# A hybrid decoder layer on one core: q's transposes, the planner's POOL prices and slab releases, and the sums of the last norm

## The chip, the core and the metric

The kernel runs on one core of a Trainium2 (trn2) chip. The metric is the device time of one execution in microseconds (us); runs are compared by their median. The engines are TensorE (PE: matmuls, and PEld for its weight loads), VectorE (DVE), ScalarE (ACT), GpSimd (POOL) and SyncE (SP), which here only issues DMAs.

## The reference

One layer for 1024 tokens of width 1024, in float32:

```python
h   = rmsnorm(x, norm_mix_w)
p   = h @ w_in                       # q, k, v, z (4 heads x 128), a, b, lru_x, lru_gate
q, k, v = silu(causal_conv4(qkv));  q = l2norm(q);  k = l2norm(k)
o   = gated_delta_rule_chunked(q, k, v, g, beta)
o   = rmsnorm(o, gdn_norm_w) * silu(z)
lru = rg_lru(causal_conv4(lru_x)) * gelu(lru_gate)
x   = x + concat(o, lru) @ w_out
u   = relu(rmsnorm(x, norm_mlp_w) @ w_ff1)
x   = x + (u * u) @ w_ff2
out = rmsnorm(x, final_norm_w)
```

The chunked delta rule needs, per head, the inverse of a unit lower triangular matrix built from k, and then a scan over chunks whose state is a 128x128 matrix. The l2 norm of q is not applied to q: its sum of squares per token goes into the norm of the output o.

## The kernel before, in words

All data lie transposed, with channels on the partitions and tokens along the row, in two halves of 512 tokens (hf 0 and 1). Float32 precision in the big products comes from splitting each operand into a high and a low part, three matmuls of 128x512 for each 128x128 block of weights (tiles w, xh and xl; results pj in the first projection, po in the second, pf and p in the MLP).

The stages are the input norm, the first projection (with the four heads and the recurrent channels woven in), the second projection, and the MLP, which forms its products from sums and differences of blocks in fewer multiplications.

Nothing is issued while the layer is written down. Every call is recorded in a `Plan` as an operation with its reads and writes, and `Plan.emit` (L285) then sets the order: it keeps a clock of its own for each engine, gives each operation a price (`price`, L264), adds a lag between engines, and at each step issues the operation that can start first, by its due time among those that start about equally early. So the order on each engine is fixed before the kernel runs, and an instruction that the planner thought ready can hold up everything behind it on that engine if its input is late. All instructions carry the line of the one call that issues them (L376); rows are told apart by their tiles. Three things of the planner matter here:

- `admit` (L296) adds `SLACK` to the ready time of a PE operation with a due time from 30 to 1000 (the small ones of the heads) that depends on another engine.
- A POOL step is priced by its row length n: `return 0.2 + 0.0021 * n` (L283).
- The on-chip buffers are 84 slabs of 128x512 float32 (tag "s") and 8 PSUM banks (tag "m"). When the last user of a tile has been placed, its slab goes back at the planner's end of that user plus 0.2 (L382). A tile that takes the slab next then waits, in the kernel, for that last user.

One head goes through these functions: `gd_k` (k transposed by PE into psK, squares and a scaled copy kd on ACT), `gd_u` (psA = k k^T on PE, U on DVE), `invert32` and `rows32` (the 32x32 diagonal blocks go by way of DRAM into the slabs N0 and N1; POOL works through them in 31 rounds of a product into tm and a difference on V, of which the first 16 read N0 and the rest N1; the result goes by way of DRAM into Y), `gd_inv` (32x32 blocks of Y transposed on DVE into YT, then small matmuls psP, psZ and psT double the block size), `gd_q` (psB = k q^T, at on DVE, and q transposed into psQ by four PE transposes per half so that ACT can sum squares per token into pn), `gd_v` (v transposed by `turn`) and `gd_scan` (matmuls pvs and psO, eight chunks one after another). The tile n1B is the scale of the input norm: DVE multiplies each finished pj by it into p, which frees pj's PSUM bank; y is then the convolution on DVE.

`turn` (L671) transposes 128x512 without PE: a DVE transpose of 32x32 blocks, four DMAs to DRAM that put the blocks in their places, and one DMA back. Before the change it is used for v and for o.

At the end, the last two blocks of 256 tokens of the MLP's output are finished in PE groups of p; for each, DVE adds p into u (tile u), ACT squares (sq), and `normed` sums five tiles of squares over the channels with matmuls by ones (n3p: the four new ones and ss, the squares of the other half of the channels), two 128x1 outputs for each tile and each matmul two instructions; then come a square root and its correction (n3r, ms, rst), its broadcast by PE (n3b), eight DVE products into ot and the DMAs of outT.

Of the kernel before, what the change touches and what calls it, by code (L numbers as in the profile page):

```python
# [13 lines left out]
P = 128  # L14
# [18 lines left out]
LOOK = 4  # L33
AHEAD = 100
TAIL = 4
SLACK = 1.3
LAND = 2.0
LATE = 2.5
SMALL = ("bv", "tr")
# [29 lines left out]
def lag(a, b):  # L69
    return LAG[a, b] if (a, b) in LAG else LAG_FROM[a] + (0.12 if b == "pe" else 0.0)  # L70
# [114 lines left out]
class Plan:  # L185
# [77 lines left out]
    @staticmethod  # L263
    def price(e, method, args, kw):  # L264
        out = kw.get("out", args[0] if args else None)
        src = [v for k, v in kw.items() if isinstance(v, View) and k in ("in_", "in0", "in1", "data0")]
        shape = out.shape if isinstance(out, View) else src[0].shape
        n = 1
        for d in shape[1:]:
            n *= d  # L270
        if e == "sy":
            return n * shape[0] * 4 / 300e3
        psum = any(v.root.tag == "m" for v in src)
        ptr = sum(isinstance(kw.get(k), View) for k in ("scalar", "scalar1", "scale", "bias"))
        if e == "ve":
            if method == "reciprocal":
                return 0.06 + 0.0066 * n
            return 0.067 + n * (0.00104 if method in TWO or psum else 0.00052) + 0.06 * ptr
        if e == "ac":
            return 0.0008333 * n + (0.051 if psum else 0.094) + 0.093 * ptr + (0.093 if "accum_out" in kw else 0.0)  # L280
        if method == "memset":
            return 0.036 + 0.00083 * n
        return 0.2 + 0.0021 * n  # L283

    def emit(self, engines, caps):  # L285
        ops = self.ops
# [6 lines left out]
        slots = {t: [(0.0, k) for k in range(n)] for t, n in caps.items()}  # L293
        table, dma = None, 0.0

        def admit(o):  # L296
            for e in o.engines:
                late = SLACK if e == "pe" and o.due < 1000.0 and o.due > 30.0 else 0.0
                ready[e].append((max([d.end + lag(d.eng, e) + (late if d.eng != "pe" else 0.0) for d in o.deps], default=0.0), o))

        def loads(o):

            return o.table is not None and o.table != table and not (o.table == "any" and table in WITH_TANH)
# [44 lines left out]
        for _ in range(len(ops)):  # L348
            pick = choose(True) or choose(False)
            if pick is None:  # L350
                left = [o for o in ops if o.eng is None and not o.wait]
                raise RuntimeError("no room: " + ", ".join(f"{o.engines}.{o.calls[0][0]}:{[r.nm for r in o.roots if r.real is None]}" for o in left[:30])
                                   + str({t: len(s) for t, s in slots.items()}))
            e, s, o = pick
            for x in o.engines:
                ready[x] = [q for q in ready[x] if q[1] is not o]
            for r in o.roots:
                if r.real is None:
                    sl = slots[r.tag]
                    r.slot = max((x for x in sl if x[0] <= s), default=min(sl))  # L360
                    sl.remove(r.slot)
                    r.real = r.make(r.slot[1])
            c = o.cost[e]
            if e == "sy":
                small = any(r.tag in SMALL for r in o.roots)
                free[e] = s + (0.62 if small else 0.45)
                dma = max(dma, free[e] + 0.65) + c
                o.end = dma + (LATE if small else LAND)
            else:
                if loads(o):  # L370
                    table = "exp" if o.table == "any" else o.table
                    c += LOAD
                free[e] = o.end = s + c
            o.eng = e
            for method, args, kw in o.calls:
                getattr(engines[e], method)(*[v.ap() if isinstance(v, View) else v for v in args],  # L376
                                            **{k: v.ap() if isinstance(v, View) else v for k, v in kw.items()})
            for r in o.roots:
                r.users -= 1
                r.end = max(r.end, o.end)  # L380
                if not r.users:
                    slots[r.tag].append((r.end + 0.2, r.slot[1]))  # L382
            for q in o.next:
                q.wait -= 1
                if not q.wait:
                    admit(q)
# [4 lines left out]
def layer(ctx: ExitStack, tc: tile.TileContext, xT, win, wba, prm, cst, wga, wgx, wout, w1, w2, out):  # L391
# [3 lines left out]
    pl = Plan()  # L395
    pe, ve, ac, gp, sy = (pl.engine(n) for n in engines)
# [9 lines left out]
    def slab(nm, dt=F32):  # L406
        return pl.tile(sp, [P, 512], dt, "s", nm)
# [4 lines left out]
    def bank(nm):  # L412
        return pl.tile(mpool, [P, 512], F32, "m", nm)

    def small(nm, shape, bufs=2, dt=F32):
        caps[nm] = bufs
        n = 4
        for d in shape[1:]:
            n *= d
        return pl.tile(cp if n % LINE else bp, shape, dt, nm, nm)  # L420
# [44 lines left out]
    def con(nm):  # L465
        o, w = CST[nm]
        return cs[:, o:o + w]

    ident = con("ident")
# [71 lines left out]
    def when(i):  # L541

        return 14.0 * i
# [127 lines left out]
    def turn(x, nm):  # L671

        y = slab(nm + "t")
        ve.transpose(out=y.rearrange("p (a x) -> p a x", x=32), in_=x.rearrange("p (a x) -> p a x", x=32))
        d = pl.tile(dpool, [P, 512], F32, "tr", nm + "d", True)
        dv = d.rearrange("(j r) (c i x) -> r c j i x", r=32, c=4, i=4)
        for i in range(4):
            sy.dma_start(out=dv[:, :, :, i, :], in_=y[32 * i:32 * i + 32].rearrange("p (c j x) -> p c j x", c=4, j=4))
        z = slab(nm)
        sy.dma_start(out=z, in_=d)  # L680
        return z
# [62 lines left out]
    def gd_q(h, hf):  # L744
        S = HD[h]
        EG, DT = S["qg"][hf], S["DT"][hf]
        kT, qT = store[4 + h, hf], store[h, hf]
        psB = bank("psB")
        with pl.unit(0.86):
            for c in range(4):  # L750
                ks = slice(c * P, (c + 1) * P)
                pe.matmul(psB[:, ks], lhsT=kT[:, ks], rhs=qT[:, ks], start=True, stop=True)
        at = S["at"][hf] = slab("at")
        ve.tensor_tensor(out=at, in0=psB, in1=DT, op=ALU.mult)
        S["last"] = S.get("last", []) + [pl.ops[-1]]
        ve.tensor_tensor(out=EG, in0=EG, in1=qT, op=ALU.mult)
        psQ = bank("psQ")
        with pl.unit(0.44):
            for c in range(4):
                pe.transpose(psQ[:, c * P:(c + 1) * P], qT[:, c * P:(c + 1) * P], ident)  # L760
        pn = S["pn"]
        for c in range(4):
            n = hf * 4 + c
            ac.activation(out=small("osq", [P, P], 2), in_=psQ[:, c * P:(c + 1) * P], func=AF.Square, accum_out=pn[:, n:n + 1])
        if hf == 1:
            ve.tensor_scalar(out=pn, in0=pn, scalar1=EPS, scalar2=EPS * P, op0=ALU.add, op1=ALU.mult)
# [236 lines left out]
    with pl.at(due=-2000.0):  # L1003
        for hf in range(2):
            hs = slice(hf * 512, hf * 512 + 512)
            ps0 = [bank(f"g0_{i}") for i in range(2)]
            ss = slab("ss1")
            for k in range(KT):
                pl.due = -2000.0 + 10 * k + 100 * hf
                if hf == 0:  # L1010
                    xraw[0, k] = slab("xraw")
                    sy.dma_start(out=xraw[0, k], in_=xT[k * P:(k + 1) * P, hs])
                    if k in (0, 2, 4):
                        n = 4 if k == 4 else 2
# [101 lines left out]
    ss = pair("ss2")  # L1116
# [31 lines left out]
    for n, d in enumerate(DO):  # L1148
        i = len(MT) + n
        t = when(i)  # L1150
        split(i + 1)
        for hf in range(2):
# [6 lines left out]
            with chain(t + 7 + 7 * hf):  # L1159
# [3 lines left out]
                x = bm[d, hf] = slab("bm")  # L1163
# [55 lines left out]
    for g in range(NG):  # L1219
        t = tf(g)  # L1220
        ps, y = {}, {}
# [121 lines left out]
    def plus(x, y):  # L1343
        ve.tensor_tensor(out=x, in0=y, in1=x, op=ALU.add)
# [40 lines left out]
    def squares(x, n=512):  # L1385
        y = slab("sq3")[:, 0:n]
        ac.activation(out=y, in_=x, func=AF.Square)
        return y
# [6 lines left out]
    for st, prods in enumerate(STAGES):  # L1395
        tail = TAIL if st == 3 else 0
        pd = {}
        for g0 in range(0, NG, 2):
# [6 lines left out]
            for d in range(4):  # L1405
                for i in prods:
# [10 lines left out]
                    with chain(ts(st, g0) - 100):  # L1417
                        if i in (1, 7, 5):
                            x = {1: p1, 7: u3, 5: p5}[i][d] = slab(f"p{i}_")
# [10 lines left out]
            for x, k, g in residual[st]:  # L1430
                if g in gs:
                    with chain(ts(st, g) + 3):
                        plus(x[k[0] % 4], load_x2(*k, st, g))
                        if x is p5:
                            y = squares(p5[k[0] % 4])
                            if k[0] == 4:
                                ss = y
                            else:
                                plus(ss, y)
        t = begin[st] + 87  # L1440
# [7 lines left out]
        if st == 2:  # L1448
            with chain(t - 40):
                s1 = None  # L1450
                for x in [p1[d] for d in range(4)] + [u3[d] for d in range(4)]:
                    y = squares(x)
# [6 lines left out]
    t = ts(3, NG - TAIL)  # L1459
# [5 lines left out]
    for o in (0, 256):  # L1465
        qs = slice(o, o + 256)
        parts = []
        for d in range(4):
            ps = bank("p2")[:, 0:256]
            for g in range(NG - TAIL, NG):  # L1470
                with pl.at(due=10000.0 + t + o / 50 + 0.1 * d), pl.unit(PIECE / 2):
                    mm3(ps, wsl(g, 3, d), tuple(x[:, qs] for x in UU[g, 3]), g == NG - TAIL, g == NG - 1)
            with chain(t - 100):
                x = u2[d][:, qs]
                plus(x, ps)
                parts.append((squares(x, 256), t))
        parts.insert(1, (ss[:, qs], t))
        X = [u2[d][:, qs] for d in range(4)] + [p5[d][:, qs] for d in range(4)]
        normed(X, parts, 512 + o, 256, t + o / 50, [4, 5, 6, 7, 0, 1, 2, 3], True)

# [64 lines left out]
```

## Time and profile before

| | us |
|---|---|
| median of 3 runs | 1110.3 |
| runs | 1108.43, 1110.3, 1110.89 |
| the profiled execution | 1107.9 |
| its span in the trace | 1105.8 |
| PE busy | 1087.3 |
| DVE busy | 864.8 |
| ACT busy | 552.1 |
| POOL busy | 100.5 |

The mean granted clock of PE over the span is 0.993 of full speed. "Busy" counts time in which an engine works on an instruction; it says nothing of the clock, so a PE at half clock is busy too. The rest of the profile is in the rows below.

### The profile page before, as it was taken

What the parts mean: (1) busy time and instruction counts of PE and PEld (TensorE: products, weight loads), DVE (VectorE), ACT (ScalarE), POOL (GpSimd) and SP (SyncE); (2) the same over time, 40 slices, a digit from 0 to 9 for tenths busy, and PEclk for the clock granted to TensorE, in tenths of its full rate; (3) what the DMA queues carried; (4) which work ended last, traced back from release to release, by engine and by line L of the source; (5) the groups of instructions that cost most, each with busy time, mean ns of one, the idle gap of its engine ahead of it and who ended that gap; (6) DMA issues with size and microseconds to landing.
All of it is one profiled execution on the core that took longest, in us unless ns stands there. A gap on an engine that the chain in (4) does not pass through costs nothing. (4 is left out here: it accounts for less than half of the span.)

```text
span 1105.8 us, 15998 instructions
## 1 busy us (share of the span) xinstructions
PE 1087.3 (98%) x5399; PEld 895.7 (81%) x5399; DVE 864.8 (78%) x1672; ACT 552.1 (50%) x1134; POOL 100.5 (9%) x282
## 2 busy tenths in 40 slices
PE   9999989999999999999999999999999999999996
PEld 7788867888787878888888888888888888888886
DVE  7878665797779776598988888887965767865796
ACT  8559634545485955453333333333444544564442
POOL 0004857026000000000000000000000000000000
PEclk9999989999999999999999999999999999999998
DMA  7133513233212144424544444434856565677382
GB/s 239 39 96 86 125 27 103 68 89 97 78 58 58 39 152 133 153 95 147 197 146 158 146 160 143 171 140 174 283 179 220 180 206 184 206 237 241 125 296 84
DMA packets 124225, 159.17 MB, mean 144 GB/s; under 512 B 56392, under 2 KB 59120, under 8 KB 124144
## 3 DMA queue, kind: packets, MB, share of 16 engines
q1 hardware_dynamic: 124144, 158.16, 44.3%
q8 instruction: 42, 0.69, 0.3%
q14 instruction: 39, 0.32, 0.1%
HBM read 115.11 MB, written 43.01 MB: 143 GB/s over the span
## 5 line engine op out<-in xcount | busy, mean ns | idle before, releaser
L376 PE MATMUL pj<-xh,w 128*128 128x512 f32 x704 | 244.9, 406 | 0.5 <-DVE p L376 0.5
L376 PEld LDWEIGHTS pj<-xh,w 128*128 128x128 f32 x704 | 133.1, 189 | 28.6 <-DVE p L376 1.1
L376 PE MATMUL pj<-xl,w 128*128 128x512 f32 x352 | 138.2, 393 | 0.0
L376 ACT ACTIVATE c<-c 128x512 f32<-128x512 f32 x64 | 40.4, 632 | 85.6 <-DVE c L376 80.7
L376 PE MATMUL po<-mxh,w 128*128 128x512 f32 x256 | 79.3, 390 | 0.8 <-ACT mxh L376 0.8
L376 ACT CAST w<-r 128x512 fp32r<-128x512 f32 (+1 forms) x62 | 51.3, 828 | 54.7 <-PE pf L376 37.8
L376 DVE SCALAR_TENSOR_TENSOR y<-p,pr,y 128x512 f32<-128x512 f32 (+3 forms) x96 | 71.5, 750 | 6.5 <-ACT y L376 4.1
L376 PEld LDWEIGHTS pj<-xl,w 128*128 128x128 f32 x352 | 66.9, 190 | 10.5
L376 DVE TENSOR_TENSOR w<-r,w 128x512 fp32r<-128x512 f32 (+1 forms) x62 | 58.7, 947 | 19.2 <-ACT w L376 18.8
L376 POOL TENSOR_TENSOR tm<-V,N 128x60 f32<-128x60 f32 (+24 forms) x124 | 48.4, 390 | 128.6 <-DMA N<-bn 69.3
L376 PEld LDWEIGHTS po<-mxh,w 128*128 128x128 f32 x256 | 48.0, 188 | 11.1 <-ACT mxh L376 1.2
L376 PE MATMUL po<-mxl,w 128*128 128x512 f32 x128 | 49.9, 390 | 0.7 <-DVE mxl L376 0.7
L376 POOL TENSOR_TENSOR V<-V,tm 128x60 f32<-128x60 f32 (+24 forms) x124 | 45.3, 365 | 9.7
L376 DVE SCALAR_TENSOR_TENSOR c<-c,n2B 128x512 f32<-128x512 f32 x64 | 43.8, 689 | 1.2
L376 PE MATMUL pf<-B5h,w 128*128 128x512 f32 x128 | 42.7, 394 | 0.0
L376 PE MATMUL pf<-B6h,w 128*128 128x512 f32 x128 | 42.3, 390 | 0.0
L376 ACT ACT_TABLE_LOAD x27 | 34.6, 1283 | 3.5 <-DVE y L376 2.4
L376 DVE TENSOR_TENSOR c<-pf,u 128x512 f32<-128x512 f32 x48 | 32.8, 686 | 0.5
L376 ACT CAST v6h<-s 128x512 fp32r<-128x512 f32 x16 | 10.0, 622 | 41.0 <-DVE s L376 41.0
L376 PEld LDWEIGHTS pf<-B5h,w 128*128 128x128 f32 x128 | 24.0, 188 | 6.9 <-DVE c L376 2.0
L376 PE MATMUL p<-u3h,v3h 128*128 128x512 f32 (+1 forms) x80 | 28.4, 355 | 0.7 <-DVE u L376 0.7
L376 PEld LDWEIGHTS po<-mxl,w 128*128 128x128 f32 x128 | 24.0, 188 | 6.0 <-DVE mxl L376 1.0
(512 smaller groups left out, 2976.2 us busy)
## 6 DMA issues: line engine op xcount, KB each, us to landing
w2r<-w SPq DMA_DIRECT2D x112, 256.0 KB, 3.5
ur<-ud SPq DMA_DIRECT2D x112, 256.0 KB, 4.9
r<-w SPq DMA_DIRECT2D x32, 512.0 KB, 3.7
ud<-c SPq DMA_DIRECT2D x64, 256.0 KB, 2.1
ud<-ut SPq DMA_DIRECT2D x48, 256.0 KB, 2.1
r<-win SPq DMA_DIRECT2D x22, 512.0 KB, 4.0
xraw<-xT SPq DMA_DIRECT2D x16, 256.0 KB, 5.2
r<-wout SPq DMA_DIRECT2D x8, 512.0 KB, 4.5
```

Source lines behind the costliest of these rows:

```text
L376: getattr(engines[e], method)(*[v.ap() if isinstance(v, View) else v for v in args], **{k: v.ap() if isinstance(v, View) else v for k, v i ...
```

## The change

It has four parts. `SLACK` becomes 1.0. A POOL step is priced at 0.22 + 0.0023 n. A slab whose last user is on POOL or SP is given back 2.0 after that user's planned end, where it was 0.2. In `gd_q` the four PE transposes into psQ are replaced by `turn`, with the tiles qct (DVE), qcd (DRAM) and qc (back on chip), so that ACT reads squares from a slab. And in the last norm, per block of 256 tokens, the first new square tile takes ss, and then the second and third squares, by three DVE additions; two tiles instead of five go through n3p.

```diff
-SLACK = 1.3
+SLACK = 1.0
...
-        return 0.2 + 0.0021 * n
+        return 0.22 + 0.0023 * n
...
-                    slots[r.tag].append((r.end + 0.2, r.slot[1]))
+                    slots[r.tag].append((r.end + (2.0 if e in ("gp", "sy") else 0.2), r.slot[1]))
...
-        psQ = bank("psQ")
-        with pl.unit(0.44):
-            for c in range(4):
-                pe.transpose(psQ[:, c * P:(c + 1) * P], qT[:, c * P:(c + 1) * P], ident)
+        psQ = turn(qT, "qc")
...
-                parts.append((squares(x, 256), t))
-        parts.insert(1, (ss[:, qs], t))
+                y = squares(x, 256)
+                if d == 0:
+                    plus(y, ss[:, qs])
+                    parts.append((y, t))
+                elif d < 3:
+                    plus(parts[0][0], y)
+                else:
+                    parts.append((y, t))
```

Since prices, waits and buffers feed the planner, the order changes on every engine. Three places follow. In these rows a name in brackets after "waits" is the engine whose count the instruction waits for, and DMAHW with a number is a queue of DMAs.

DVE in the first projection, where the second half of head 0's Y is transposed into YT while POOL works on head 1. Before:

```order
L376 STREAM_TRANSPOSE YT<-Y_0_824 128x256 [waits DMAHW2_49,DMAHW0_49]
L376 SCALAR_TENSOR_TENSOR y_1614<-p,pr,y_1614 128x512 [waits DVE_49] x2
L376 STREAM_TRANSPOSE YT<-Y_1_835 128x256 [waits DMAHW4_49,DMAHW6_49,DMAHW1_49,Pool_49]
L376 TENSOR_TENSOR p<-pj_1586,n1B 128x512 [waits DVE_49,PE_49]
L376 COPY YP<-psP 32x128 [waits PE_49]
```

The same place after; rst, rk, sk and cj are the small factors of head 2, and qct is the new transpose of its q:

```order
L376 STREAM_TRANSPOSE qct<-y_1650 128x512
L376 TENSOR_TENSOR rst<-rk 128x8 [waits DVE_49]
L376 COPY YP<-psP 32x128 [waits PE_49]
L376 SCALAR_TENSOR_TENSOR rst<-rst,sk 128x8 [waits DVE_49]
L376 COPY YP<-psP 32x128
L376 SCALAR_TENSOR_TENSOR rk<-rst,rk 128x8 [waits DVE_49]
L376 STREAM_TRANSPOSE YT<-Y_1_853 128x256 [waits DMAHW6_49,DMAHW0_49]
L376 TENSOR_TENSOR rst<-rk 128x8 [waits DVE_49]
L376 TENSOR_TENSOR p<-pj_1630,n1B 128x512 [waits PE_49]
L376 SCALAR_TENSOR_TENSOR rst<-rst,sk 128x8 [waits DVE_49]
L376 TENSOR_TENSOR at<-psB,DT 128x512 [waits DMAHW7_49,PE_49,Pool_49]
```

The transpose of Y no longer waits for POOL: its slab is another one. The slab that POOL reads as N0 of head 1 now goes to the tile at of head 2, four rows further on, so the wait for POOL stands there, behind the p that frees a PSUM bank.

PE where small matmuls of several heads stand together between two runs of the projection (pj). Before:

```order
L376 MATMUL psK<-cs,y_2523 128x128 [waits DVE_49,PE_49,Activation_49]
...
L376 MATMUL psA<-y_2523 128x128 x4
L376 MATMUL pvs<-vs,Y_0_1484 128x128
L376 MATMUL psT<-cs,Y_0_1901 64x64 [waits DMAHW1_49,DVE_49]
...
L376 MATMUL pvs<-vh,kd 128x128 [waits DVE_49]
L376 MATMUL psO<-vh,at 128x128
L376 MATMUL psP<-YT,U_1_1834 32x32 [waits DVE_49]
...
L376 MATMUL pj_2677<-xh_247,w 128x512 [waits Activation_49]
```

The place in the order after that has the most such waits with no pj between:

```order
L376 MATMUL psK<-cs,y_2277 128x128 [waits DVE_49,Activation_49]
...
L376 MATMUL pvs<-S,y_528 128x128 [waits DVE_49]
L376 MATMUL psO<-S,qg 128x128
L376 MATMUL psA<-y_2277 128x128 [waits DVE_49]
...
L376 MATMUL pvs<-vs,Y_1_853 128x128 [waits DVE_49]
L376 MATMUL psZ<-Y_1_1531,YT 64x64 [waits DMAHW7_49,Activation_49]
...
L376 MATMUL pvs<-vs,Y_0_1516 128x128 [waits DVE_49]
L376 MATMUL pvs<-vh,kd 128x128 [waits DVE_49]
L376 MATMUL psO<-vh,at 128x128
L376 MATMUL pj_2450<-xh_107,w 128x512 [waits DVE_49]
```

From psK to the row ahead of pj seven instructions wait for DVE, ACT or a DMA, where four did before. A line of three dots stands for the further rows of the same matmul.

PE at the end. Before, the last group of p is cut by n3p:

```order
L376 MATMUL n3p<-onesd,sq_11114 128x1 [waits Activation_49]
...
L376 MATMUL p_11106<-u3h,v3h 128x256
L376 MATMUL p_11106<-u3l,v3h 128x256
L376 MATMUL p_11106<-u3h,v3l 128x256
L376 MATMUL n3p<-onesd,sq_11136 128x1 [waits Activation_49]
...
L376 MATMUL n3b<-cs,n3r 128x128 [waits DVE_49,Activation_49]
```

And after:

```order
L376 MATMUL p_11102<-u3h,v3h 128x256
L376 MATMUL p_11102<-u3l,v3h 128x256
L376 MATMUL p_11102<-u3h,v3l 128x256
L376 MATMUL n3p<-onesd,sq_11096 128x1 [waits DVE_49,Activation_49]
...
L376 MATMUL n3b<-cs,n3r 128x128 [waits DVE_49]
...
L376 MATMUL n3p<-onesd,sq_11144 128x1 [waits Activation_49]
...
L376 MATMUL n3b<-cs,n3r 128x128 [waits DVE_49,Activation_49]
```

Both blocks' n3b now stand behind the last p; before, the first block's stood ahead of it, and its eight products into ot ran beside the last p.

## Rows read from the trace of the kernel before

**Rows 1.** The page's part 1: span, then busy us (share) and instructions per engine.

```profile
span 1105.8 us, 15998 instructions
PE 1087.3 (98%) x5399; PEld 895.7 (81%) x5399; DVE 864.8 (78%) x1672; ACT 552.1 (50%) x1134; POOL 100.5 (9%) x282
```

**Rows 2.** Waits of PE: who waited for whom, us in total, times, longest.

```profile
PE psA L376 <- DVE p L376: 3.8, 1, 3.8
...
PE n3b L376 <- DVE n3r L376: 1.4, 1, 1.4
...
PE psP L376 <- DVE S L376: 0.7, 1, 0.7
```

**Rows 3.** Windows: length, busy us of each engine, PEclk, DMA share, GB/s.

```profile
125.00:150.00 25.00, 21.23 (x133) 16.89 (x132) 13.54 (x27) 10.75 (x39) 20.60 (x63) 0.81 0.27 68
200.00:225.00 25.00, 24.25 (x194) 20.38 (x193) 18.23 (x53) 13.04 (x52) 0.00 (x0) 1.00 0.27 66
500.00:700.00 200.00, 200.00 (x883) 164.38 (x882) 173.18 (x281) 76.47 (x129) 0.00 (x0) 1.00 0.46 161
```

**Rows 4.** Finer windows around 140 to 151 us, same columns.

```profile
140.00:141.00 1.00, 0.00 (x0) 0.00 (x0) 0.00 (x0) 0.00 (x0) 0.84 (x3) 0.87 0.00 0
...
147.00:150.00 3.00, 3.00 (x23) 2.33 (x22) 2.35 (x10) 0.66 (x2) 2.45 (x8) 0.50 0.02 5
150.00:151.00 1.00, 1.00 (x18) 0.48 (x16) 0.00 (x0) 0.01 (x1) 0.77 (x4) 0.51 0.00 0
```

**Rows 5.** Timeline of PE: start us, us, instruction, [idle before <-releaser].

```profile
138.58 0.60 PE L376 MATMUL psK<-cs,y 128*128 128x128 f32 x4
142.94 1.44 PE L376 MATMUL psA<-y 128*128 128x128 f32 x5 [3.77 <-DVE p L376]
```

**Rows 6.** Timeline of DVE at the same place.

```profile
135.76 1.61 DVE L376 SCALAR_TENSOR_TENSOR y<-p,pr,y 128x512 f32<-128x512 f32 x2
141.87 0.45 DVE L376 STREAM_TRANSPOSE YT<-Y 128x256 f32<-128x256 f32 x1 [4.49 <-POOL tm L376]
142.24 0.65 DVE L376 TENSOR_TENSOR p<-pj,n1B 128x512 f32<-128x512 f32 x1
```

**Rows 7.** Timeline of POOL at the same place.

```profile
141.53 0.30 POOL L376 TENSOR_TENSOR tm<-V,N 128x64 f32<-128x64 f32 x1
```

**Rows 8.** Instructions on psQ: duration ns min/median/max, first and last start us.

```profile
L376 PE MATMUL psQ<-cs,y x32: 272/273/329, 79.4 to 244.5; 128*128 128x128 f32 x32
```

**Rows 9.** Timeline of PE at a transpose of the same form.

```profile
130.50 0.60 PE L376 MATMUL psK<-cs,y 128*128 128x128 f32 x4
130.94 1.06 PE L376 MATMUL psA<-y 128*128 128x128 f32 x8
```

**Rows 10.** Instructions of v's `turn`, columns as in rows 8.

```profile
L376 SPq DMA_DIRECT2D vsd<-vst x32: 569/627/799, 58.4 to 261.3; - x32
L376 DVE STREAM_TRANSPOSE vst<-y x8: 697/705/711, 57.7 to 258.0; 128x512 f32<-128x512 f32 x8
...
L376 SPq DMA_DIRECT2D vs<-vsd x8: 326/430/557, 64.0 to 265.5; - x8
```

**Rows 11.** The reader of pn at the end of a half's scan.

```profile
L376 DVE SCALAR_TENSOR_TENSOR ro<-so,pn x8: 152/160/164, 194.5 to 366.9; 128x4 f32<-128x4 f32 x8
```

**Rows 12.** The chain that ended last: start us, us, what.

```profile
1088.26 2.13 PE n3p L376 x20
...
1092.82 0.44 PE n3b L376 x4
...
1098.63 0.17 DVE n3r L376
```

**Rows 13.** Timeline of DVE at the end.

```profile
1095.98 0.42 DVE L376 TENSOR_TENSOR u<-p,u 128x256 f32<-128x256 f32 x1
...
1099.65 0.42 DVE L376 TENSOR_TENSOR ot<-n3b,p__9670 128x256 f32<-128x256 f32 x1 [0.86 <-PE n3b L376]
1099.99 0.41 DVE L376 TENSOR_TENSOR ot<-n3b,p__9702 128x256 f32<-128x256 f32 x1
...
1100.99 1.65 DVE L376 SCALAR_TENSOR_TENSOR ot<-u,pr,n3b 128x256 f32<-128x256 f32 x4
```

**Rows 14.** Timeline of PE among small matmuls.

```profile
218.92 0.49 PE L376 MATMUL pvs<-vh,kd 128*128 128x128 f32 x2
...
220.29 0.44 PE L376 MATMUL psP<-YT,U 32*32 32x32 f32 x16 [0.66 <-DVE S L376]
```

## The prediction, written before the changed kernel ran

> **What bounds the kernel now.** I read the page's first part, the waits of PE, the clock by windows, and then the timelines of the three engines at the one long wait. PE is busy 1087.3 of a span of 1105.8 us [rows 1], and in the MLP it is busy 200.00 of 200 us at a granted clock of 1.00 [rows 3]. So time comes from four sources only: work taken off PE, idle time of PE, PE's clock, and the end, where PE has finished. DMAs, loads and stores that move about in the MLP cost nothing as long as PE stays at 200 of 200 there, and I put that reordering at 0.
>
> The idle time is nearly one event. Of the waits of PE the longest by far is psA for DVE's p, 3.8 us [rows 2]. At that place PE ends psK at 139.2 and starts psA at 142.94 [rows 5]. It wants the PSUM bank that p frees; p stands on DVE behind the second transpose into YT, and that waited 4.49 us for POOL's tm [rows 6]. The POOL step at 141.53 is the last round that reads N0 of head 1 [rows 7], and YT sits in the slab that was N0: DVE waited for a buffer, not for data. During the idle time the clock fell: the windows give 0.87 for 140 to 141 us, 0.50 for 147 to 150, and 0.51 for 150 to 151 [rows 4]. So PE worked from 142.94 to about 150.98 at 1.2 GHz, the lower of its two levels, 8.04 us whose work takes half as long at 2.4. The event costs 3.77 + 4.02 = 7.8 us.
>
> **The change part by part.**
>
> *q's transposes.* 32 transposes leave PE [rows 8]. Their 273 ns overlap; four of the same form take 130.94 - 130.50 = 0.44 us from the first to the next work [rows 9]. Eight sets give 8 x 0.44 = 3.5 us off a PE that is otherwise busy in that stage. What comes in: 8 DVE transposes of 0.705 us, 5.6 us in all, and on SP 32 x 0.63 + 8 x 0.43 = 23.6 us of issuing [rows 10]. DVE is busy 13.5 to 18.2 of 25 us in this stage [rows 3], so the 5.6 us, spread over some 170 us, lie in its idle time; the bound is 5.6 if every one stood on PE's path. The squares are read late: the first of q's transposes ran at 79.4, the first reader of pn runs at 194.5 [rows 8, 11], so a landing some us later is covered. ACT's squares read a slab in place of PSUM; ACT is busy 10.8 to 13.0 of 25 us there [rows 3], so a change in their length is hidden. SP has room, about 24 us more over 170, but its queue runs in order and loads of weights and the bn, N and Y copies stand behind q's. I take 0 for the queue; its upper bound is inside the rival on starved PE below.
>
> *Prices and slab releases.* By the order, YT no longer waits for POOL, and p comes ahead of the tile at that now does. I take the whole event away: -3.8 for the idle time and -4.0 for the clock. What is late next at this place is at: it takes the slab that POOL reads until 141.8 in the trace of before; the longer release puts it further behind that, but by how much in time the order doesn't say.
>
> *The smaller `SLACK`.* Small PE work is placed 0.3 us closer behind DVE and ACT, so it may find its input late. The trace of before shows what such a wait costs when it comes: 0.66 us at psP [rows 14]. Nearest row below: that wait goes, -0.7; above: one such wait more for each head, 4 x 0.7 = 2.8. I take one, +0.7, because rows 2 hold just one of that kind in four heads.
>
> *The last norm.* n3p falls from 40 to 16 instructions; 20 took 2.13 us, 0.107 each [rows 12], so 24 are 2.6 us of PE. Not all of it reaches the end, since DVE takes over. Before the last p there were 36 n3p and four n3b instructions (0.44 us), now 8 and none: the last p comes 28 x 0.107 + 0.44 = 3.4 us earlier, and with it the last u, from 1095.98 to about 1092.6 [rows 13]. The three additions per block, about 0.34 to 0.42 each by the spacing and length of DVE's 128x256 products [rows 13], run while PE does p. But behind the last u now stand both blocks' products. From u (0.4) over one small step (0.2) to n3r 1093.2; from n3r to the first ot the old tail took 1099.65 - 1098.63 = 1.0 [rows 12, 13], so 1094.2. Then eight products, 4 x 0.34 + 4 x 0.41 = 3.0, with six small steps of the other block between them at 0.2, 1.2 in all: 1098.4. The other n3b is ready by then (n3r stands three products earlier, 1.2 against 1.0), and the last eight take 3.0: 1101.4 to 1101.5, where it was 1100.99 + 1.65 = 1102.64. Gain 1.1. Bounds: 0, if DVE's steps wait for ACT's squares in turn, and 2.6, the work itself.
>
> *The sum,* on the profiled execution of 1107.9 us (span 1105.8 and 2.1 around it): -3.5 - 3.8 - 4.0 + 0.7 - 1.1 = -11.7, so 1096.2. That execution was 2.4 us below the median of the runs shown, 1110.3; against the median the forecast is 1110.3 - 11.7 = 1098.6.
>
> **The rivals.**
>
> *The wait moves to at.* The order shows at waiting for POOL on the same slab, four rows on. For it: POOL's rounds take as long as ever, and DVE, no longer held at YT, comes there earlier. Against it: p is ahead of at, so the bank that starved PE is free; and the longer release and price both push at back. Behind at on DVE stand the small factors rk, cj and sk of head 2, and psB's bank is held until at has run, so PE's next user of that bank and psA's reader wait for it. If PE starves behind at as it did behind YT, the 7.8 us come back: 1098.6 + 7.8 = 1106.4.
>
> *The clock falls without a long wait.* In the trace, idle times of 0.66 us among small matmuls went with a granted clock of 1.00 over the whole 25 us [rows 3, 14], and only the 3.77 us one went with a fall. If a run of short waits did pull the clock down, the place shown in the order after, with seven waits between psK and pj, is where: 7 x 0.7 = 4.9 of idle in place of the 0.7, and one slow stretch like that of rows 4, 4.0: -11.7 - 0.7 + 4.9 + 4.0 = -3.5, 1106.8. The Trainium skill, "TensorE: Matmul & The Clock Gate", section "A second HAM failure mode: psum-queue depth-cycling", speaks for this one: it says that frequent tiny idles between groups of matmuls can make the clock swing between its levels. By that rule the reordered place costs 8 us more than by rows 3 and 14, which show four such waits and a clock of 1.00; the trace so far speaks against it here, so its chance is small.
>
> *PE starves at that place (slower).* The seven waits are steps of two heads' chains, DVE to PE and back, and DVE has the splits w, the products zs and q's transposes of 0.7 us in the same queue. If the first of them grows to the longest wait shown, 3.8, and the other six to the next kind, 1.4 [rows 2], it is 12.2 of idle and 4.0 of slow clock, 16.2 in place of 0.7: -11.7 + 15.5 = +3.8, 1114.1. It decides from 14.6 us on (11.7 + 0.7 and the 2.2 that can be told). Against it: before, the place with four such waits lost 0.66 in all.
>
> *Nothing is left.* The wait at at and the short idles together, 7.8 + 8.2 - 4.0 for a clock that is low already, take back the whole: 1110.3.
>
> **How the numbers follow.** Forecast 0.66, wait at at 0.14, clock 0.06, nothing left 0.06, starved PE 0.08. A measurement tells 0.2%, about 2.2 us, from no change. Faster by more than that: 0.66 + 0.14 + 0.06 = 0.86; within it 0.06; slower 0.08. The forecast's own range runs from everything better (-3.5 - 7.8 - 0.7 - 2.6 = -14.6, 1095.7) to the waits at 2.8 and no gain at the end (-8.5, 1101.8). The spread of the runs, 1108.43 to 1110.89, adds 1.9 below. With the two cases near 1106.5 the range is 1094 to 1107; it leaves out starved PE, nothing left and some of the edges, under 2 in 10.
>
> **What would show it.** PE with about 5343 instructions (32 + 24 fewer); no wait of psA for p over 1 us; no wait of DVE's YT for POOL; a clock of 1.00 in 125 to 150 us; eight transposes qct of 0.7 us; the last ot about 8.2 us after the last u, where it was 6.7. Wrong would be: a wait of PE over 3 us at psP or pj, a clock under 1.00 before the tail, or DVE's at waiting for POOL by more than 1 us.

## The result and the profile after

| | before | after |
|---|---|---|
| median of runs, us | 1110.06 | 1098.88 |
| runs, us | 1108.43 to 1110.89 | 1096.62 to 1099.74 |
| profiled execution, its span, us | 1107.9, 1105.8 | 1096.62, 1094.6 |
| ratio, 95% interval | | 0.9898, 0.9879 to 0.9917 |

The forecast was 1098.6. The page's first part, against [rows 1]: PE has 56 instructions fewer, as 32 transposes and 24 matmuls n3p have gone, and DVE has more.

```profile
span 1094.6 us, 15988 instructions
PE 1077.7 (98%) x5343; PEld 887.7 (81%) x5343; DVE 868.2 (79%) x1686; ACT 557.1 (51%) x1138; POOL 101.4 (9%) x282
```

The waits of PE, against [rows 2]: psA's wait of 3.8 for p is gone. The longest is now in the tail; apart from one of 1.5 us at the very start that both have, the rest are 1.2 or less.

```profile
PE n3b L376 <- DVE n3r L376: 2.7, 2, 2.3
...
PE psZ L376 <- ACT kd L376: 1.2, 1, 1.2
```

Windows, with the columns of [rows 3]: the clock is 1.00 where it was 0.81, and the idle time of that window is 0.06 us where it was 3.77. The second window holds the place that I had feared.

```profile
125.00:150.00 25.00, 24.94 (x168) 20.49 (x167) 19.48 (x44) 15.45 (x49) 21.07 (x57) 1.00 0.48 100
...
175.00:200.00 25.00, 23.55 (x191) 19.18 (x191) 16.90 (x45) 10.79 (x41) 18.71 (x53) 1.00 0.45 114
```

DVE's timeline at the second YT, against [rows 6], and POOL's at the last round on N0 of head 1, against [rows 7]:

```profile
144.75 0.43 DVE L376 STREAM_TRANSPOSE YT<-Y 128x256 f32<-128x256 f32 x1
...
145.26 0.69 DVE L376 TENSOR_TENSOR p<-pj,n1B 128x512 f32<-128x512 f32 x1
...
145.95 0.68 DVE L376 TENSOR_TENSOR at<-psB,DT 128x512 f32<-128x512 f32 x1
```

```profile
144.10 0.30 POOL L376 TENSOR_TENSOR tm<-V,N 128x64 f32<-128x64 f32 x1
```

POOL ended its last read at 144.40, and at came to its slab 1.55 us later, without a wait.

PE at the place with seven waits: one of them waited, and the pj behind them, 1.17 + 0.28 = 1.45 us in all, at full clock.

```profile
195.42 0.43 PE L376 MATMUL pvs<-vs,Y 128*128 128x128 f32 x2
197.02 0.67 PE L376 MATMUL psZ<-Y,YT 64*64 64x64 f32 x8 [1.17 <-ACT kd L376]
...
198.83 0.50 PE L376 MATMUL pj<-xh,w 128*128 128x512 f32 x1 [0.28 <-DVE Y L376]
```

DVE's tail, against [rows 13]: from the last u to the end of the last product 1089.74 + 1.64 - 1083.10 = 8.3 us, where it was 6.7.

```profile
1083.10 0.42 DVE L376 TENSOR_TENSOR u<-p,u 128x256 f32<-128x256 f32 x1 [0.33 <-PE p L376]
...
1088.41 0.42 DVE L376 TENSOR_TENSOR ot<-n3b,p__9702 128x256 f32<-128x256 f32 x1 [0.20 <-PE n3b L376]
...
1089.74 1.64 DVE L376 SCALAR_TENSOR_TENSOR ot<-u,pr,n3b 128x256 f32<-128x256 f32 x4
```

By stages: the second products of the MLP start with the same matmul in both traces. Before, and after:

```profile
782.75 0.39 PE L376 MATMUL p<-u1h,v1h 128*128 128x512 f32 x1
```

```profile
773.27 0.39 PE L376 MATMUL p<-u1h,v1h 128*128 128x512 f32 x1
```

So 9.5 us came from the projection with the heads. The last u, which follows the last p, is 12.9 us earlier (1095.98 in [rows 13], 1083.10 now), so PE's share of the norm is 3.4. The last product ends 11.3 earlier (1102.64, 1091.38), so DVE's longer tail gave 1.6 of that back and the norm's part gained 1.8.

One execution of 1927 us, of the kernel with a release of 3.0 below, is left out of that kernel's ratio.

### The profile page after: what moved, and what is told of

It reads as the page before. It is cut to its first block, busy times and chain, and to the rows that moved or that the text cites. A ratio compares the mean times of both kernels' runs of the same rounds, so it can differ in the third digit from the quotient of the medians.

```text
span 1094.6 us, 15988 instructions
## 1 busy us (share of the span) xinstructions
PE 1077.7 (98%) x5343; PEld 887.7 (81%) x5343; DVE 868.2 (79%) x1686; ACT 557.1 (51%) x1138; POOL 101.4 (9%) x282
```

## The experiments

Times of one group are held against runs of the kernel before on the same chip: a median of 1109.4 for b_ytslab, b_fill, b_norm and a_rel; 1109.6 for b_qturn, b_order, a_price and a_slack; 1110.9 for a_norm, a_dblk, a_s08 and a_rel3. Ratios are to these, with 95% intervals; the changed kernel has 0.9898.

**Another slab for YT, in the kernel before (b_ytslab).**

```diff
-                    r.slot = max((x for x in sl if x[0] <= s), default=min(sl))
+                    r.slot = min(sl) if r.nm == "YT" else max((x for x in sl if x[0] <= s), default=min(sl))
```

> The kernel before, with one thing altered: tiles named YT take the slab that has been free longest, not the one freed last. The order on PE and DVE stays as it was, and the YT of head 0's second half no longer waits for POOL. Theory (the 7.8 us were a wait for a buffer, 3.8 of idle PE and 4.0 of slow clock): about 1102.3 where before has 1110.1, no wait of psA for p over 1 us and a clock of 1.00 from 125 to 150 us. Since POOL's rounds stay where they are, a later instruction of DVE that waits for POOL (at of head 2) may come early and give back up to 3 us: 1102 to 1105.5. Rival (it was the order as a whole, and any other buffer only moves the wait a few rows on): within 2 us of before.

1104.92, ratio 0.9965 (0.9952 to 0.9977). The order is the same and YT no longer waits, yet PE still waited 2.84 us, and the clock was 0.50 from 147 to 150. ACT's timeline and PE's tell where the wait went:

```profile
142.06 0.72 ACT L376 ACTIVATE y<-p,pr 128x512 f32<-128x512 f32 x1 [3.51 <-POOL tm L376]
```

```profile
141.40 0.44 PE L376 MATMUL psZ<-Y,YP 32*32 32x32 f32 x16
146.26 0.64 PE L376 MATMUL psZ<-Y,YP 32*32 32x32 f32 x16 [2.84 <-DVE rk L376]
```

A tile y of the convolution, which reads nothing of POOL's, waited 3.51 us on ACT until POOL's round (begun at 141.73) was done. ACT's squares of psK and DVE's next y stood behind it, and PE ran dry one step later. So it was a wait for a buffer, and the rival is half right: with YT elsewhere, the next tile in line waited for POOL instead. That y had drawn YT's former slab is concluded from the releaser that the trace names; no row names slabs.

**Filling PE's idle time, in the kernel before (b_fill).**

```diff
-            for c in range(4):
+            for c in list(range(4)) * (6 if (h, hf) == (2, 1) else 1):
                 pe.transpose(psK[:, c * P:(c + 1) * P], kT[:, c * P:(c + 1) * P], ident)
```

> The kernel before, with the four PE transposes of k into psK done six times over, for head 2's second half alone: those just ahead of the long wait. It adds 20 transposes, 20 x 0.11 = 2.2 us of PE work, inside the 3.77 us in which PE waited, and the rest of the order is that of before. Theory (half of the loss was the clock, which fell because PE stood idle): PE's idle time there falls to about 1.6 us, the clock stays at 1.00, psA starts at the same time, and 4.0 us are gained: about 1106. Rival (the clock falls for another reason, or the 8 us of work after it were slow for lack of data): no change, 1110.

1107.33, but the ratio, 0.9990 (0.9977 to 1.0003), can't be told from no change. In the profiled execution the idle time fell to 1.73 us, from 143.1 to 144.8, and the clock fell later and for less long, but it fell:

```profile
140.00:145.00 5.00, 3.27 (x28) 2.90 (x27) 1.21 (x3) 0.18 (x2) 3.99 (x13) 1.00 0.00 0
...
147.00:150.00 3.00, 3.00 (x23) 2.06 (x22) 2.79 (x10) 2.14 (x10) 2.47 (x7) 0.50 0.02 5
150.00:152.00 2.00, 2.00 (x24) 1.19 (x23) 1.15 (x7) 0.42 (x1) 1.61 (x6) 0.95 0.00 0
```

By the medians the theory's 4.0 us were not had. But five of the 12 executions, the profiled one not among them, have a mean clock of 0.996 or 0.997 and took 1104.97 to 1106.87, the theory's 1106, while none of the 26 executions of the kernel before has more than 0.994. So with less idle time the clock's loss is smaller in some executions, and in others it stays.

**The last norm alone, in the kernel before (b_norm).** The edit is the last part of the diff.

> The kernel before with the last norm's part of the change alone; the order differs at the very end only. Forecast before the result: 1.1 us gained, as PE ends 3.4 us earlier and DVE's tail gets longer. By the trace of after (last u 3.4 us earlier against the start of the second products, last product 8.3 after it where it was 6.7): 1.8 us gained, 1108.3. Rival (all work taken off PE counts): 2.6 to 3.4, 1107. Rival (DVE's additions sit on the path): 0 or below.

1106.37, ratio 0.9972 (0.9961 to 0.9983), so 3.1 us, more than the tail's 1.8, which its trace shows again (3.5 from PE's last p, 1.6 given back). The next run, which puts the old norm back into the changed kernel, shows where a part of the rest can lie.

**The old norm in the changed kernel (a_norm).** The same part of the diff, undone.

> The changed kernel with the last norm as before (five tiles of squares through n3p); the order differs at the very end only. Theory (the norm's part is worth 1.8 us by the tail and, in some executions, a fall of the clock that follows the 40 small matmuls n3p): 2 to 4 us slower than the changed kernel, 1101 to 1103, the last product in the trace 1.8 us later against the start of the second products. Rival (PE's work alone, 24 x 0.107): 2.6 in every execution, no fall of the clock between 1080 and 1095 us.

1100.98, ratio 0.9919 (0.9897 to 0.9940): 2 us slower than the changed kernel by the ratios, whose intervals overlap. Of five executions three took about 1100.9 with 4.4 us lost to the clock (1 less its mean, times the span), and two 1105.6 with 11.0 lost. The changed kernel's profile lost 4.4 too, all of it behind 1083 us, where the last p had ended. The profile here is of one of the two slower executions. PE's timeline and windows:

```profile
1082.16 0.28 PE L376 MATMUL p<-u3h,v3l 128*128 128x256 f32 x1
1082.28 2.29 PE L376 MATMUL n3p<-onesd,sq 128*128 128x1 f32 x20
...
1084.87 1.40 PE L376 MATMUL n3p<-onesd,sq 128*128 128x1 f32 x8
...
1086.48 0.41 PE L376 MATMUL p<-u3l,v3h 128*128 128x256 f32 x1
```

```profile
1084.00:1086.00 2.00, 2.00 (x17) 2.00 (x16) 0.96 (x6) 0.48 (x2) 0.00 (x0) 0.80 0.00 0
1086.00:1088.00 2.00, 2.00 (x11) 2.00 (x11) 0.43 (x1) 0.39 (x1) 0.00 (x0) 0.50 0.00 0
```

PE was busy throughout and the clock fell all the same, behind 20 matmuls of 128x1 in a row, three of p, and the first of eight more of 128x1. A p of 128x256 takes 0.41 us behind them and 0.28 ahead. At this place the clock cost 0.2 x 2 + 0.5 x 6 = 3.4 us. That is about half of the 6.6 by which the two sorts of execution differ. The rest of this profile's loss lies far ahead of the norm, where the order is the changed kernel's: the mean clock is 0.79 from 30 to 38 us (1.7 us lost) and 0.57 from 201 to 205 (1.7 lost), behind the very place that I had feared:

```profile
198.68 0.68 PE L376 MATMUL psZ<-Y,YT 64*64 64x64 f32 x8 [1.02 <-ACT kd L376]
...
200.63 0.50 PE L376 MATMUL pj<-xh,w 128*128 128x512 f32 x1 [0.40 <-DVE Y L376]
```

```profile
201.00:205.00 4.00, 4.00 (x15) 3.32 (x14) 1.96 (x7) 2.77 (x11) 3.10 (x14) 0.57 0.56 185
```

Where the other execution of 1105.6 lost its time is not recorded. Of the five other kernels profiled with 40 n3p than the one before, four show a fall ahead of the last p, at the n3p (a_norm, b_fill, b_qturn and b_order; not b_ytslab), in one execution each; the profile of before does not, and of the kernels with 16, none does. So the norm's part is worth 1.8 us, and up to 3.4 more in those executions in which the clock would fall there.

**q by `turn` alone, in the kernel before (b_qturn).** One line of the diff.

> The kernel before with q's part of the change alone. By the order none of DVE's YT and at waits for POOL any more, though prices, SLACK and releases are those of before. Theory (terms add: 3.5 us off PE, and the long wait goes with the buffer, of which the kernel with other YT slabs kept 4): -7.5, about 1102. Rival (the long wait belongs to prices, SLACK and releases): -3.5, about 1105.9, and PE still waits some 3 us at one place between 130 and 150 us.

1107.49, ratio 0.9983 (0.9970 to 0.9996): 2 us, less than either theory. The long wait is gone, but the order has another dry place. The waits of PE and the windows:

```profile
PE pvs L376 <- DVE vs L376: 2.4, 2, 1.3
...
PE pj L376 <- DVE vh L376: 1.2, 1, 1.2
```

```profile
125.00:150.00 25.00, 24.41 (x180) 19.30 (x179) 20.13 (x49) 16.51 (x50) 21.07 (x57) 1.00 0.42 102
...
220.00:225.00 5.00, 2.50 (x40) 2.11 (x41) 4.86 (x16) 1.00 (x3) 0.00 (x0) 0.76 0.38 102
225.00:230.00 5.00, 5.00 (x19) 4.01 (x18) 3.94 (x20) 1.18 (x7) 0.00 (x0) 0.56 0.49 174
```

At 220 to 225 DVE is busy 4.86 of 5 us and PE 2.50, and the clock falls in that stretch.

**The planner's three numbers alone, in the kernel before (b_order).** The first three lines of the diff.

> The kernel before with the three numbers of the planner alone (SLACK, POOL's price, release); q goes through PE. By the order the YT of head 0's second half does not wait for POOL, two YT of later heads do. Theory (the three numbers take the long wait away): -4 to -7, 1102.4 to 1105.4, and a clock of 1.00 from 125 to 150 us. Rival (the wait went because q's transposes moved buffers and DVE's work): within 2 us of before.

1105.17, ratio 0.9950 (0.9931 to 0.9969): 4.4 us by the medians, 5.5 by the ratio, within the theory's 4 to 7. The long wait is gone here too, so either half of the change takes it away:

```profile
125.00:150.00 25.00, 24.80 (x191) 20.21 (x190) 17.14 (x43) 12.27 (x43) 20.84 (x60) 1.00 0.26 62
```

**The changed kernel with the old release (a_rel).**

```diff
-                    slots[r.tag].append((r.end + (2.0 if e in ("gp", "sy") else 0.2), r.slot[1]))
+                    slots[r.tag].append((r.end + 0.2, r.slot[1]))
```

> The changed kernel with slabs given back 0.2 after every last user, as before. The order shows the transposes YT of head 0's second half and of head 1's first half waiting for POOL again. Theory (what counts is by how much DVE comes ahead of POOL's last read; in the trace of after DVE reached that YT at 144.75 when POOL's last read had begun at 144.10 and taken 0.3): the wait is near zero and the time within 1.5 us of the changed kernel, 1098.9. Rival (the longer release is what removed the event): the 7.8 us come back, about 1106.5.

1107.13, ratio 0.9984 (0.9970 to 0.9998): 8 us lost, as the rival had it, but not where it had it. The YT that the order shows waiting for POOL ran at 145.24 without a wait. The time went at 208 to 233 us, PE's timeline and the windows:

```profile
209.12 0.63 PE L376 MATMUL psK<-cs,y 128*128 128x128 f32 x4 [0.43 <-DVE p L376]
...
212.07 0.49 PE L376 MATMUL pvs<-S,y 128*128 128x128 f32 x2 [1.43 <-ACT kd L376]
...
213.93 0.80 PE L376 MATMUL pvs<-vs,Y 128*128 128x128 f32 x2 [1.14 <-DVE vs L376]
215.17 0.80 PE L376 MATMUL pvs<-vh,kd 128*128 128x128 f32 x2 [0.44 <-DVE vh L376]
```

```profile
210.00:213.00 3.00, 1.35 (x10) 0.97 (x9) 2.63 (x11) 2.02 (x12) 0.44 (x1) 1.00 0.20 31
213.00:215.00 2.00, 0.80 (x2) 0.50 (x2) 1.01 (x6) 0.00 (x0) 0.00 (x0) 0.60 0.44 74
...
220.00:225.00 5.00, 5.00 (x19) 3.64 (x17) 3.51 (x11) 2.30 (x6) 0.00 (x0) 0.50 0.55 95
225.00:230.00 5.00, 5.00 (x23) 3.60 (x23) 2.89 (x18) 1.24 (x8) 0.00 (x0) 0.50 0.13 20
230.00:235.00 5.00, 5.00 (x30) 3.81 (x29) 2.41 (x11) 0.15 (x1) 0.00 (x0) 0.61 0.23 62
```

Four waits of 0.43 to 1.43, 3.4 us in all; the clock falls within the third of them and stays at 1.2 GHz for about 20 us. PE was busy for some 19.5 of these, so the clock cost some 9.8 us (an estimate: half of that). No single wait is longer than 1.43 us. The profiled execution, 1109.8, is one of the slower: the 12 range from 1104.47 at a mean clock of 0.994 to 1111.44 at 0.988.

**The changed kernel with the old price, and with other numbers (a_price, a_slack, a_s08, a_rel3).** The edits are `0.2 + 0.0021 * n`; `SLACK = 1.3` and `0.8`; and 3.0 in place of the release of 2.0.

> The changed kernel with POOL's old price, 0.2 + 0.0021 n. By the order the first YT of head 1 waits for POOL. Theory (the dearer price is what keeps DVE behind POOL's last reads: some 94 rounds' steps at 0.03 are 3 us): DVE waits up to 3 us for POOL at that YT, and 0 to 4 us are lost against the changed kernel, 1099 to 1103. Rival (the price matters by the order alone): no wait of DVE for POOL over 1 us, and whatever is lost or gained stands at short waits of PE elsewhere.

> The changed kernel with SLACK 1.3. Theory of the prediction (the smaller number lets small PE work find its input late, one more wait of 0.7; the stage with the heads showed 1.9 us more of short idle times than before): 0.7 to 1.9 us faster than the changed kernel, 1097 to 1098. Rival (each order has starved places of its own, and which one has none is chance): 3 us or more slower, with a run of short waits or a slow clock somewhere between 100 and 350 us.

> The changed kernel with SLACK 0.8. Theory (each order has starved places of its own; the number acts by which order comes out, not by its size): the time lies anywhere from 1097 to 1108, and what is lost or gained against the changed kernel stands at runs of short waits of PE between 100 and 350 us with the clock that falls behind them. Rival (smaller is better, as 1.0 was 3 us better than 1.3): 1 to 2 us faster, 1097.

> The changed kernel with slabs given back 3.0 after a last user on POOL or SP. Theory (as for SLACK: by the order that comes out): 1097 to 1108, the difference at runs of short waits and the clock behind them. Rival (the longer the release, the fewer the waits for POOL's slabs; 2.0 was 8 us better than 0.2): the same or up to 1 us faster, 1098 to 1099, with no wait of DVE for POOL.

| | median, us | ratio (interval) |
|---|---|---|
| old price | 1098.72 | 0.9901 (0.9885 to 0.9918) |
| SLACK 1.3 | 1102.23 | 0.9928 (0.9914 to 0.9942) |
| SLACK 0.8 | 1096.39 | 0.9872 (0.9854 to 0.9890) |
| release 3.0 | 1107.84 | 0.9975 (0.9963 to 0.9987) |

The price is worth nothing that the runs can tell: the YT named in the expectation did not wait, one other tile on DVE (vst) waited 1.0 us for POOL, and the time is the changed kernel's. `SLACK` 1.3 costs some 3 us, and 0.8 has the fastest median of all; the intervals of both overlap the changed kernel's at the edge, so neither difference is settled. The theory of a lost wait per step of `SLACK`, by which 1.3 would be faster, has the sign against it. A release of 3.0 is as bad as 0.2, so "the longer the better" is refuted, and the loss is again short waits from 205 to 220 us with the clock down behind them:

```profile
205.00:215.00 10.00, 7.63 (x60) 6.21 (x58) 7.72 (x25) 3.19 (x10) 1.06 (x2) 0.89 0.31 51
215.00:220.00 5.00, 4.55 (x25) 3.55 (x24) 2.12 (x7) 1.91 (x4) 0.00 (x0) 0.50 0.74 139
220.00:230.00 10.00, 10.00 (x36) 7.54 (x35) 6.51 (x27) 2.65 (x8) 0.00 (x0) 0.50 0.38 87
```

With `SLACK` 1.3 PE waits 0.67, 0.39 and 1.26 us between 193 and 198, and the clock is 0.65 from 195 to 200 and 0.50 from 200 to 205. With 0.8 no wait between the start and the tail is over 1.2 us, and the profiled execution is at full clock up to there.

**PE's transposes of k done twice, in the changed kernel (a_dblk).**

```diff
-            for c in range(4):
+            for c in [0, 1, 2, 3] * 2:
                 pe.transpose(psK[:, c * P:(c + 1) * P], kT[:, c * P:(c + 1) * P], ident)
```

> The changed kernel with every set of PE transposes of k into psK done twice over, in all eight half heads, at the same places of the order: 8 x 0.44 = 3.5 us of PE work of the kind that q's transposes were, and nothing else. Theory (PE bounds this stage, so such work counts in full): 3.5 us slower than the changed kernel, 1102.4. Rival (part of it falls into PE's idle times, 3.8 us of them between 30 and 390 us): 1 to 2.5. Rival (it feeds later work late): over 4.5.

1100.85, ratio 0.9908 (0.9892 to 0.9925): 1.1 us by the ratios, 2.0 by the medians. In the traces it is 3.1 from the 100th pj to the start of the second projection (4.4 in all, of which 1.4 stand before the first transpose, where the clock's mean is 0.73 from 30 to 36 us and the changed kernel's profile is at full clock). So this sort of PE work counts nearly in full in one trace, 3.1 of 3.5; by the runs, between nothing and 3, which leaves the theory and the first rival both standing.

## Why the prediction was right, point by point

*The long wait and its clock, -7.8: right, and for the reason given, with a gap in it.* It is gone in the trace, and the clock is 1.00. Either half of the change takes it away (b_order, b_qturn), and it stays away when the release or the price alone goes back (a_rel, a_price). b_ytslab shows that it was a wait for the buffer that POOL read, but also that giving YT another buffer is not enough: the next to draw that slab waits (y, 3.51 us). The rival "the wait moves to at" described what happens in that kernel, with another tile. In the changed kernel at drew the slab and came 1.55 us after POOL's last read. I had no number for that margin.

*q's transposes, -3.5: not contradicted.* a_dblk's trace has 3.1, its runs allow less.

*The stage's sum.* -3.5 - 7.8 and the short waits make the 9.5 us that came from there. I had put +0.7 for short waits. By the two traces, from 30 to 380 us and without the long wait, idle times of over 0.2 us are 3.8 after and 1.7 before: about +2.

*`SLACK`: the step that failed.* I took the smaller number for the cause of more short waits. 1.3 came out some 3 us slower than 1.0, and 0.8 no slower. The short waits went with q's `turn`: counted as above, in one profile each, idle times are 1.7 us before, 2.0 with the planner's three numbers alone (b_order), 6.3 with q by `turn` alone (b_qturn) and 3.8 with both; with `SLACK` 1.3 they are 4.6 and with 0.8 they are 3.1. I had put q's transposes down as free on DVE and the queue; which of `turn`'s steps makes PE wait stays open.

*The last norm, -1.1: the mechanism right, two sizes off.* PE's 3.4 us are what was measured. The tail behind the last u is 8.3 us; my own times made it 8.8 (the 8.2 in the list of signs was a slip), so the gain is 1.8. And I did not see that 20 matmuls of 128x1 in a row can cost the clock though PE is busy.

*The clock without a long wait: the rival that I priced rightly and believed too little.* I gave it 0.06 because [rows 3, 14] showed a clock of 1.00 at a place with four instructions that wait. But only one of them had been late, by 0.66 us, so these rows said nothing of a run of short waits. a_rel, a_rel3, b_qturn and a_slack show the clock fall among short waits that follow each other closely, and a_rel's 8 us are near what I had for such a place (4.9 and 4.0). The Trainium skill, "TensorE: Matmul & The Clock Gate", section "A second HAM failure mode: psum-queue depth-cycling", describes a kernel in which frequent tiny idles between groups of matmuls make the clock swing between its levels. a_rel's trace agrees in that the clock fell among idles of 0.43 to 1.43 us; it shows one slow stretch of 20 us, not a swing. The changed kernel's order does not always escape it: in its own profile the feared place had 1.45 us of waits at full clock, but in a_norm's, with the same order there, 1.42 us of waits were followed by a fall that cost 1.7. Two of the changed kernel's four executions have a mean clock of 0.994 (1099.33 and 1099.74) and two of 0.996 (1096.62 and 1098.44), which is some 2 us between them, so a small form of this rival may stand in the measured median. That it stayed small is partly luck: nothing in the trace of before told it.

So the sum was met partly by offsets: 1.3 too little for short waits, 0.7 too little for the tail, and the clock's share, which varies: 26 executions of the kernel before range from 1107.12 at a mean clock of 0.994 to 1112.43 at 0.988. What stays open is how much each part is worth in general: b_order, b_qturn and b_norm gain 5.5, 1.9 and 3.1 us by their ratios, 10.5 together where the whole has 11.3, but undoing the release alone loses 8.

## What to carry to other kernels

When a planner fixes the order, read a removed wait as "whoever draws this buffer next": find that instruction in the new order and ask by how much it comes after the last read. One number of a planner can change the order on every engine, so measure a few neighbours of it before a gain is put down to the number. Price a run of short waits with the clock that may fall behind it, not by its idle time alone. And take a difference between two profiles for the kernel's only after looking where the clock fell in each: the same order can lose time in one execution and not in another.

## What the runs showed of the hardware that was not expected

The clock of PE fell while PE's records showed no idle time, behind a row of matmuls with an output of 128x1 (0.80 from 1084 to 1086 us, then 0.50, in a_norm's profile), and not in every profile with these matmuls: neither in that of before nor in b_ytslab's. The same instructions in the same order, after waits of about the same length, were at full clock in one execution and not in another: 1.00 from 200 to 205 us in the changed kernel's profile, 0.57 from 201 to 205 in a_norm's. And the same long wait goes with different slow stretches. In the profiled execution of before the fall comes within the wait and the stretch lasts about 10 us; in b_norm's, with the same order and an idle time that is as long, it comes only behind the wait, and the mean for 125 to 150 us is 0.88 where it was 0.81:

```profile
125.00:150.00 25.00, 21.13 (x135) 16.60 (x133) 13.37 (x27) 10.65 (x39) 20.75 (x61) 0.88 0.22 52
```
